# An encoder block on one core: output weights' last quarter read and summed beside branch A's merge, tokens' low parts behind the first blocks' results, gate weights read ahead of head one

## The chip, the core and the metric

The kernel runs on one core of a Trainium2 chip. The core has five engines that run side by side and meet through semaphores: TensorE (PE in the profile) for matrix products, VectorE (DVE), ScalarE (ACT), GpSimd (POOL), and SyncE (SP), which here only issues DMA transfers. Each engine works through its own instructions in order. The metric is device time in microseconds (us) of the whole program.

## The reference

One encoder layer over 1024 tokens and 16 meta tokens put ahead of them, width 1024, in float32:

```
h   = concat(meta, x)
p   = rms_norm(h) @ w_in                    # qa, ka, va, qb, kb, vb, gate a, gate b
y_a = differential attention, 4 heads       # two softmaxes subtracted, per-head norm
y_b = windowed attention, 8 heads, 2 key/value heads, window 128, sinks
m   = sigmoid(ga) * (y_a @ w_branch_a) + sigmoid(gb) * (y_b @ w_branch_b)
h   = h + m @ w_out
h   = h + (silu(n @ w_gate) * (n @ w_up)) @ w_down      # n = rms_norm(h), inner width 2816
out = rms_norm(h), without the meta tokens
```

## The kernel before, in words

Every matrix product is made of float32 values split in two: ACT copies the value into a rounded "high part" (line 112) and VectorE or POOL subtracts that from the value for the "low part" (line 113). Three products (high by high, high by low, low by high) then stand for one in float32. A product of 512 columns by 128 contracted rows is three matmuls, and four contracted chunks make twelve, summed in one PSUM bank.

The stages follow each other on TensorE: projections and windowed attention; the heads of differential attention, with the gate projections filling in between; branch B's merge and branch A's merge; the output projection; the feed-forward network, up and down. The order on TensorE is the program's order in most stages (`manual_schedule`). On the other engines and on SP's queue of transfers, a planner decides it when the kernel is compiled; buffers of a pool are handed on as their readers finish.

*The merges (from line 859).* For each of eight columns of 128 outputs (`o`) and each half of the tokens, `gated` reads the stored gate from DRAM into one of four buffers (`GT_BUFS`), ACT applies the sigmoid (line 862), and TensorE multiplies branch weights by the branch's result (line 551). VectorE then multiplies gate and product (line 874 in branch B, 899 in branch A), and in branch A POOL adds that to branch B's share (line 900). `branch_w` reads one column of branch weights into a raw tile of a ring of five (`RING_RAW`) and splits it into one of seven buffers (`WB_BUFS`). `order_a` is the order of branch A's sixteen outputs. The banks of PSUM alternate between two groups of four (`ps_bank`, `ps_bank_t`).

*The output projection* uses seven products in place of eight (Strassen's scheme in Winograd's form). For it the four quarters of `w_out` are read as W11, W12, W21 and W22, and turned in place into the sums that the scheme needs: T2 = W22 - W11 (line 1110), W12 := W22 - W12 (line 1164), W21 := W21 - T2 (line 1166), each in four pieces of 128 by 512. W22 has its read at the eleventh output of branch A, into the space of branch A's first operand. The merged values get sums of the same kind (lines 908, 915, 916, 1162). `right_o` and `left_o` split the operands; line 1121 and line 1129 hold the matmuls.

*The feed-forward network* uses the same scheme with `product_f` (line 1218). The first four blocks run their first two products (1 and 2) ahead of the rest. `turn_f` transposes the normalised tokens and forms their sums; `split_t` splits these sums into the operands `t_5`, `t_6`, `t_7`, `t_4` of the products 5, 6, 7 and 4, at the steps that `SPLIT` names. `result` applies silu (line 1230) to the gate's product, and multiplies it by the up product (line 1235), which is what gives the product's PSUM bank free.

*The heads.* `prep` reads 128 columns of `w_in` into a buffer of two and splits them; `ensure` does so ahead for the next columns of `order`; `load_a` reads a head's operands; `fill` runs steps of the gate projections.

Of the kernel before, what the change touches and what calls it, by code (L numbers as in the profile page):

```python
# [19 lines left out]
P = 128  # L20
# [23 lines left out]
G_BUFS = 3  # L44
HOLD = 36
GT_BUFS = 4
WB_BUFS = 7
G_HEAD = 10
G_FIRST = 30

# [20 lines left out]
def encoder_block(ctx: ExitStack, tc: tile.TileContext, x, meta, norm_mix, w_in, lq1, lk1, lq2, lk2,  # L71
# [94 lines left out]

    queue = []

    def prep(col, name, p=None, lo_eng=None):
        w = wpool.tile([P, DC, P], F32, tag="w", name=f"w_{name}", bufs=2)  # L170
        nc.sync.dma_start(w, w_in[:, col:col + P].rearrange("(c p) n -> p c n", p=P))
        p, bufs = (p, 1) if p else (wpool, W_BUFS)
        wh = p.tile([P, DC, P], F32R, tag="wh", name=f"wh_{name}", bufs=bufs)
        wl = p.tile([P, DC, P], F32R, tag="wl", name=f"wl_{name}", bufs=bufs)
        split(wh, wl, w, lo_eng or nc.gpsimd)
        return wh, wl
# [530 lines left out]
    for n in range(AH * NT + T_LAG):  # L707
        scoring, turning = iter(()), iter(())
        if n < AH * NT:
            h, t = divmod(n, NT)  # L710
            if t == 0:
                if not h:
                    ensure(2)
                ld = load_a(h)
                fill(G_HEAD if h else G_FIRST)
            if t % 2 == 0:
                at_ = apool.tile([P, 9, 2, 256], F32R, tag="at", name=f"at{h}_{t}", bufs=AT_BUFS)
            s = [None, None]
            tiles.append((h, t, s, at_, ld[2]))
            scoring = scores_a(h, t, ld, s)  # L720
        if n >= T_LAG:
            turning = turn(tiles[n - T_LAG])
        for what in SLOTS if n < 3 * NT else SLOTS_LAST:
            if what == "s":
                next(scoring, None)
            elif what == "t":
                next(turning, None)
            elif what == "n":
                step_tail()
            else:  # L730
                fill(1)
        for _ in scoring:
            pass
        for _ in turning:
            pass
        if n >= T_LAG and tiles[n - T_LAG][1] % 2:
            tail.append(later(tiles[n - T_LAG]))
# [153 lines left out]
    obpools[1], close_ob = pool("obpool", "right")  # L891


    order_a = [(o, 0) for o in range(6)] + [(0, 1), (6, 0), (1, 1), (7, 0)] + [(o, 1) for o in range(2, DC)]
    for n, (o, half) in enumerate(order_a):
        if o not in ws_a:
            ws_a[o] = branch_w(ypool, o, w_ba, "a", None, nc.vector)
        gt, ps, tk = gated(1, o, half, ws_a[o], ya)
        nc.vector.tensor_tensor(gt, gt, ps, ALU.mult)
        nc.gpsimd.tensor_tensor(merged(o, half), gt, merged(o, half), ALU.add)  # L900
        if 4 <= n < 8:
            right_o(2, n - 4)
            left_o(1, n - 4)
        elif 10 <= n < 14:
            left_o(2, n - 10)
        if n in (6, 8, 10, 11):

            tt_v(a21[:, o], a11[:, o], a21[:, o], ALU.subtract)
        if n == 10:
            w22 = obpools["w22"] = block_pair(2, "m2", F32)[:, 0]  # L910
            load_wo(w22, 1, 1)
        if n >= 12:

            j = n - 12
            tt_v(asum[:, j], a22[:, j], a21[:, j], ALU.subtract)
            tt_v(a11[:, j], asum[:, j], a11[:, j], ALU.add)
# [187 lines left out]
    for i in range(2):  # L1104
        load_unit(i, 0, first_f[i])

    for j in range(4):
        if j % 2 == 0:
            t2[j // 2] = raw_tile(f"t2_{j}")
        tt_v(t2[j // 2][:, j % 2 * 512:j % 2 * 512 + 512], w22[:, j], w11[:, j], ALU.subtract)  # L1110

    order_t = ((7, 0), (7, 1), (7, 2), (4, 0), (7, 3), (4, 1), (4, 2), (4, 3))
    steps_o = [(p, j) for p in (1, 2, 6, 5, 3) for j in range(4)]
    set1 = [ps_bank(f"po_1_{u}") for u in range(4)]
# [27 lines left out]
    for n, (p, j) in enumerate(steps_o):  # L1142
        if (p, j) == (5, 0):
            sets_o[5] = sets_o[3] = [ps_bank_t(f"po_5_{u}") for u in range(4)]
        last = p in (5, 3) and j == 3
        if p in (5, 3) and j == 2:
            continue
        for u in range(4):
            for k in (2, 3) if last else (j,):
                product_o(p, k, u)  # L1150
            if (p, j) == (1, 3):

                nc.scalar.copy(set2[u], set1[u])
            elif j == 3:

                out_add(u + 4 * (p == 5), int(p > 2), sets_o[p][u])
                if p == 3:
                    norm_f(u)
        for k in (n - 1, n) if last else (n,):
            ahead(k)  # L1160
            if 4 <= k < 8:
                tt_v(a12[:, k - 4], a12[:, k - 4], asum[:, k - 4], ALU.subtract)
            elif 8 <= k < 12:
                tt_v(w12[:, k - 8], w22[:, k - 8], w12[:, k - 8], ALU.subtract)
            elif 12 <= k < 16:
                tt_v(w21[:, k - 12], w21[:, k - 12], t2[(k - 12) // 2][:, k % 2 * 512:k % 2 * 512 + 512], ALU.subtract)
    TURN_O = {2: 0, 3: 1, 4: 2, 5: 3, 6: 4}
    b11, b21, b22 = (block_pair(i, n, F32R) for i, n in enumerate(("b11", "b21", "b22")))
    for n, (p, u) in enumerate(order_t):
# [5 lines left out]
            turn_f(TURN_O[n])  # L1175
    prepare(2 * 2)
    close_late()
    close_ob()
    close_wo()
    close_keep()  # L1180
# [18 lines left out]
        for p in ps_:  # L1199
            split(t_ops[p][:, 0, :, cols], t_ops[p][:, 1, :, cols], sums_t[u][p], nc.vector)  # L1200

    st = {}

    def product_f(fp, p, i):
        op, b = ops.pop(("f", (fp, p, i))), b_ops[p]
        u = st.setdefault((i, fp), {})
        nm = f"{i}_{fp}"
        which = {1: "b1", 6: "b1", 7: "b1", 4: "b1", 2: "b2", 5: "b3", 3: "b3"}[p]
        late = N_KEPT <= fp < N_EARLY
        if p in (1, 5) or (late and p == 6):  # L1210
            u[which] = (ps_bank_t if p == 5 else ps_bank)(f"pg_{nm}_{p}")
        ps = u[which]
        if late and p == 6:

            nc.scalar.copy(ps, u[1])
        for c in range(4):
            for n, (x, y) in enumerate(((0, 0), (0, 1), (1, 0))):
                nc.tensor.matmul(ps, op[:, x, c, :], b[:, y, c, :], start=(p in (1, 5) and c == 0 and n == 0),  # L1218
                                 stop=(p in (4, 2, 3) and c == 3 and n == 2), skip_group_check=True)
        g = st.setdefault(("c", fp), {})  # L1220

        def result(key, src, other=None):

            if i == 0:

                c = g[key] = (p_tile if key == "11" and fp < N_EARLY else c_tile)(f"c_{nm}_{key}")
                if other is not None:
                    nc.vector.tensor_tensor(c, src, other, ALU.add)
                    src = c
                nc.scalar.activation(c, src, AF.Silu)  # L1230
            else:
                if other is not None:
                    nc.vector.tensor_tensor(other, src, other, ALU.add)
                    src = other
                nc.vector.tensor_tensor(g[key], g[key], src, ALU.mult)  # L1235

        if p == 1:

            u["b2"] = ps if late else ps_bank(f"pg_{nm}_2")
            if late:  # L1240
                u[1] = p_tile(f"p1_{nm}")
            nc.scalar.copy(u[1] if late else u["b2"], ps)
        elif p in (5, 6):
            u[p] = c_tile(f"p{p}_{nm}")
            nc.scalar.copy(u[p], ps)
        elif p == 2:
            result("11", ps)
        elif p == 7:
            result("22", ps, u[5])
        elif p == 3:  # L1250
            result("12", ps, u[6])
        else:
            result("21", ps)
            if i:

                a11, a21, a12, a22 = g["11"], g["12"], g["21"], g["22"]
                nc.sync.dma_start(a_d[1][fp], a11)
                s1, s2, s3, s4 = (c_tile(f"as{k}_{fp}") for k in range(1, 5))
                nc.vector.tensor_tensor(s1, a21, a22, ALU.add)
                nc.sync.dma_start(a_d[4][fp], a22)  # L1260
                nc.vector.tensor_tensor(s3, a11, a21, ALU.subtract)
                nc.sync.dma_start(a_d[7][fp], s3)
                nc.vector.tensor_tensor(s2, s1, a11, ALU.subtract)
                nc.sync.dma_start(a_d[5][fp], s1)
                nc.sync.dma_start(a_d[6][fp], s2)
                nc.vector.tensor_tensor(s4, a12, s2, ALU.subtract)
                nc.sync.dma_start(a_d[2][fp], a12)
                nc.sync.dma_start(a_d[3][fp], s4)

    TURN = {0: 5, 2: 6, 4: 7}  # L1270
    SPLIT = {2: (0, (6, 5)), 3: (1, (6, 5)), 5: (2, (6, 5)), 7: (3, (6, 5))} | {8 + u: (u, (7, 4)) for u in range(4)}
    for n in range(nf):
        prepare()
        if n in TURN:
            turn_f(TURN[n])
        if n in SPLIT:
            split_t(*SPLIT[n])
        if n == 11:
            close_h2()
            cp, close_cpool = pool("cpool")  # L1280
            cpools.append(cp)
# [157 lines left out]
```

## Time and profile before

| what | us |
|---|---|
| median of 3 runs | 1455.42 (1452.44 to 1456.17) |
| the profiled execution | 1455.01 |
| its span, first to last instruction | 1453.2 |
| TensorE busy | 1432.0 |
| VectorE busy | 893.5 |
| ScalarE busy | 675.6 |
| GpSimd busy | 471.6 |

Times in the rows are microseconds from the span's start. A row of the timeline gives the start, the duration, the engine (SPq is SP's queue of transfers), the line, the operation, the tiles written and read, their shapes and the number of instructions merged into the row; in brackets, how long the engine was idle before and what ended that. A wait gives the waiting line, what it waited for, the total, the number of times and the longest. A stretch gives busy time of each engine in it, then the clock that TensorE was granted (1.00 is full speed) and the share of the DMA engines. VectorE issues a short instruction about 0.6 us after the one before, though a row shows it as 0.67 to 0.69 us long; matmul ends are modelled.

### The profile page before, as it was taken

To read this page: it belongs to the slowest core of one execution; us is meant where nothing else is said; L and a number is where in the kernel's file an instruction comes from. 1 tells how busy PE (TensorE), PEld (TensorE's weight loads), DVE (VectorE), ACT (ScalarE), POOL (GpSimd) and SP (SyncE) were. 2 spreads that over 40 slices of the span, in tenths; PEclk is the share of its full clock that TensorE was granted. 3 is DMA by queue.
4 is the path that set the end of the run, shared out by engine and by line. 5 is a ranking of instruction groups with operands and counts; after the bars stand their busy time and mean duration, and the time that the engine had idled before them with its cause. 6 is when DMAs were issued, how large, how long until landed. Compare 5 with 4: busy or idle time off the path is not lost.

```text
span 1453.2 us, 20988 instructions
## 1 busy us (share of the span) xinstructions
PE 1432.0 (99%) x7327; PEld 1227.8 (84%) x7327; DVE 893.5 (61%) x1750; ACT 675.6 (46%) x1275; POOL 471.6 (32%) x460
## 2 busy tenths in 40 slices
PE   8999999999999999999999999999999999999997
PEld 7999989988898989888878878888888888888886
DVE  6456326627686868535777955654455543787567
ACT  6356336525554545455345844333333333444454
POOL 4143223313323232211513035454444452000444
PEclk9999999999999999999999999999999999999999
DMA  7334452373424242077341533433223333954343
GB/s 237 88 102 115 123 126 88 78 192 109 147 80 147 74 147 74 30 267 240 108 161 73 181 109 109 145 124 108 96 99 104 105 102 106 349 186 138 124 130 138
DMA packets 158618, 191.02 MB, mean 131 GB/s; under 512 B 16096, under 2 KB 103584, under 8 KB 158512
## 3 DMA queue, kind: packets, MB, share of 16 engines
q1 hardware_dynamic: 158512, 189.68, 41.1%
q8 instruction: 58, 0.95, 0.3%
q14 instruction: 48, 0.39, 0.1%
HBM read 129.14 MB, written 53.94 MB: 126 GB/s over the span
## 4 chain that ended last, share of the span: by engine, by line
PE 81%; DMA 6%; issue 4%; POOL 4%; DVE 3%; ACT 2%; SPq 1%; POOLq 0%; ACTq 0%; DVEq 0%
PE pg L1218 28%; PE pp_g L200 10%; PE pd L1314 8%; PE aps L607 4%; PE po L1121 4%; PE apy L649 3%; PE pp_va L200 3%; PE pp_ka L200 3%; PE pp_qa L200 3%; PE pp_qb L200 3%; POOL oa L113 3%; PE apt L636 2%; PE bpt L338 2%; PE bpy L344 2%; PE po L1129 2%
## 5 line engine op out<-in xcount | busy, mean ns | idle before, releaser
L1218 PE MATMUL pg<-t,wop 128*128 128x512 f32 x1056 | 242.4, 389 | 0.0
L1218 PEld LDWEIGHTS pg<-t,wop 128*128 128x128 f32 x1056 | 198.3, 188 | 41.1
L1314 PE MATMUL pd<-ob,oa 128*128 128x512 f32 x924 | 210.2, 389 | 1.2 <-DVE ob L113 0.7
L1314 PEld LDWEIGHTS pd<-ob,oa 128*128 128x128 f32 x924 | 173.3, 188 | 37.9 <-DVE ob L113 1.2
L113 POOL TENSOR_TENSOR wop<-wf,wop 128x512 fp32r<-128x512 f32 x114 | 150.4, 1320 | 165.8 <-ACT wop L112 153.9
L1218 PE MATMUL pg<-b,wop 128*128 128x512 f32 x792 | 184.2, 390 | 2.2 <-DVE c L1235 1.8
L1218 PEld LDWEIGHTS pg<-b,wop 128*128 128x128 f32 x792 | 148.2, 188 | 34.2 <-DVE c L1235 2.7
L113 POOL TENSOR_TENSOR wl_c<-w_c,wh_c 128x1024 fp32r<-128x1024 f32 x32 | 77.7, 2427 | 166.3 <-ACT wh_c L112 156.0
L112 ACT ACTIVATE wop<-wf 128x512 fp32r<-128x512 f32 x128 | 80.8, 633 | 81.4 <-PE pg L1218 53.6
L618 ACT ACTIVATE as<-as,amn 128x1040 f32<-128x1040 f32 x64 | 74.5, 1164 | 72.7 <-DVE amn L613 72.4
L200 PE MATMUL pp_g<-hT_hi,wh_c 128*128 128x512 f32 x256 | 101.3, 396 | 0.0
L200 PE MATMUL pp_g<-hT_lo,wh_c 128*128 128x512 f32 x256 | 100.9, 394 | 0.0
L200 PE MATMUL pp_g<-hT_hi,wl_c 128*128 128x512 f32 x256 | 100.9, 394 | 0.0
L113 POOL TENSOR_TENSOR oa<-ra,oa 128x512 fp32r<-128x512 f32 x33 | 44.0, 1335 | 171.1 <-ACT oa L112 169.7
L112 ACT ACTIVATE oa<-ra 128x512 fp32r<-128x512 f32 x77 | 48.7, 632 | 108.1 <-PE pd L1314 51.3
L607 PE MATMUL aps<-ak,aq 128*128 128x352 f32 (+1 forms) x384 | 92.7, 326 | 0.4 <-DVE amn L613 0.4
L990 DVE TENSOR_TENSOR s<-wf,wf 128x512 f32<-128x512 f32 x22 | 15.7, 715 | 117.0 <-DMA wf<-in_w_ff_up_dram 70.1
L607 PEld LDWEIGHTS aps<-ak,aq 128*128 128x128 f32 x384 | 69.6, 188 | 14.8 <-DVE amn L613 0.9
L613 DVE CUSTOM_DVE_ANT_0 as<-aps,dist,amn 128x352 f32<-128x352 f32 (+1 forms) x128 | 71.3, 563 | 10.2 <-PE aps L607 8.1
L325 POOL TENSOR_SCALAR bs<-bs,bdn 128x432 f32<-128x432 f32 (+1 forms) x64 | 37.0, 597 | 85.4 <-DVE bdn L323 64.1
L613 DVE CUSTOM_DVE_ANT_0 as<-aps,dist,far_a 128x352 f32<-128x352 f32 x64 | 37.1, 579 | 42.8 <-PE aps L607 42.7
L621 POOL TENSOR_SCALAR as<-as,adn,neglam 128x1040 f32<-128x1040 f32 x32 | 38.9, 1217 | 75.2 <-DVE adn L619 75.2
(270 smaller groups left out, 3040.4 us busy)
## 6 DMA issues: line engine op xcount, KB each, us to landing
ra<-aop SPq DMA_DIRECT2D x77, 256.0 KB, 2.6
w_c<-in_w_in_dram SPq DMA_DIRECT2D x33, 512.0 KB, 3.9
wf<-in_w_ff_gate_dram SPq DMA_DIRECT2D x25, 512.0 KB, 3.5
wf<-in_w_ff_up_dram SPq DMA_DIRECT2D x25, 512.0 KB, 3.6
aop<-as SPq DMA_DIRECT2D x44, 256.0 KB, 2.0
aop<-c SPq DMA_DIRECT2D x33, 256.0 KB, 2.0
g_d<-gate_stage SPq DMA_DIRECT2D x32, 256.0 KB, 2.0
gt<-g_d SPq DMA_DIRECT2D x32, 256.0 KB, 4.1
```

The source lines that it names most:

```text
L112: nc.scalar.activation(hi, src, AF.Copy)
L113: lo_eng.tensor_tensor(lo, src, f32(hi), ALU.subtract)
L200: nc.tensor.matmul(ps[:, :n], a[:, c, :], b[:, c, at:at + n], start=(c == 0 and i == 0), stop=(c == DC - 1 and i == 2))
L325: nc.gpsimd.tensor_scalar(st[:, r, :W], st[:, r, :W], dn[:, r:r + 1], 1.0, ALU.mult, ALU.mult)
L607: nc.tensor.matmul(ps[:, :n], qs[m][:, t * P:(t + 1) * P], ks[m][:, vv, k0:k0 + n], start=(vv == 0), stop=(vv == 1))
L613: nc.vector.tensor_tensor_reduce(s[m][:, a:b], ps[:, a - k0:b - k0], far_by, slope, low, ALU.add, ALU.min, mn[:, m, i + j:i + j + 1])
L618: nc.scalar.activation(s[m][:, 0:L], s[m][:, 0:L], AF.Exp, bias=low, scale=-1.0, accum_out=dn[:, m:m + 1])
L621: (nc.gpsimd if t % 4 in COMBINE_POOL else nc.vector).tensor_scalar(s[1][:, 0:L], s[1][:, 0:L], dn[:, 1:2], neglam, ALU.mult, ALU.mult)
L649: nc.tensor.matmul(py[:, cols], v[:kp, a, k, :], at_[:kp, k, b, :], start=(k == 0 and j == 0), stop=(k == 8))
L1121: nc.tensor.matmul(sets_o[p][u], oa[:, a, u * P:(u + 1) * P], ob[:, b, :], start=(p in (1, 5) and j == 0 and k == 0), stop=(p in (2, 3) an ...
L1218: nc.tensor.matmul(ps, op[:, x, c, :], b[:, y, c, :], start=(p in (1, 5) and c == 0 and n == 0), stop=(p in (4, 2, 3) and c == 3 and n == ...
L1314: nc.tensor.matmul(ps[u], oa[:, a, u * P:(u + 1) * P], ob[:, b, :], start=(p in (1, 2, 5) and j == 0 and k == 0), stop=(p in (2, 3, 4) and ...
```

## The change

There are three parts. First, W22 gets a buffer of its own (`w22`, pool `w22pool`) and is read as branch A's merge begins; the twelve sums T2, W12 and W21 are placed behind the multiplications of outputs 3 to 6 and 8 to 11 (`issue_after` puts VectorE's instructions of the block behind the one named). `WB_BUFS` goes from 7 to 6; the order of the sixteen outputs changes a little, and so do the outputs behind which `a21` is subtracted. Second, the splits of the tokens' sums no longer come at steps 2 to 11 token by token, but operand by operand, behind the last multiplication of a result (`given[-1]`): operand 6 at step 4, 5 at step 8, 7 and 4 at step 12; the second extra block takes its bank from the other group of four, and the pool `cpool` opens at step 16 instead of 11. Third, `prep` can use weights that `preload` has read, and `preload` is called for the next columns of `order` before the first head's operands are read.

```
-WB_BUFS = 7
+WB_BUFS = 6
...
+    raw_w = {}
+    def preload(col):
+        w = raw_w[col] = wpool.tile([P, DC, P], F32, tag="w", name=f"w_c{col}", bufs=2)
+        nc.sync.dma_start(w, w_in[:, col:col + P].rearrange("(c p) n -> p c n", p=P))
     def prep(col, name, p=None, lo_eng=None):
-        w = wpool.tile([P, DC, P], F32, tag="w", name=f"w_{name}", bufs=2)
-        nc.sync.dma_start(w, w_in[:, col:col + P].rearrange("(c p) n -> p c n", p=P))
+        if col not in raw_w:
+            preload(col)
+        w = raw_w.pop(col)
...
                     ensure(2)
+                    preload(order[0])
                 ld = load_a(h)
...
-    order_a = [(o, 0) for o in range(6)] + [(0, 1), (6, 0), (1, 1), (7, 0)] + [(o, 1) for o in range(2, DC)]
+    order_a = [(o, 0) for o in range(5)] + [(0, 1), (5, 0), (1, 1), (6, 0), (2, 1), (7, 0)] + [(o, 1) for o in range(3, DC)]
+    w22pool, close_w22 = pool("w22pool", "right")
+    w22 = obpools["w22"] = w22pool.tile([P, 4, 512], F32, name="w22")
+    load_wo(w22, 1, 1)
     for n, (o, half) in enumerate(order_a):
...
-        nc.vector.tensor_tensor(gt, gt, ps, ALU.mult)
+        mult = nc.vector.tensor_tensor(gt, gt, ps, ALU.mult)
         nc.gpsimd.tensor_tensor(merged(o, half), gt, merged(o, half), ALU.add)
...
-        if n in (6, 8, 10, 11):
+        if n in (5, 7, 9, 11):
             tt_v(a21[:, o], a11[:, o], a21[:, o], ALU.subtract)
-        if n == 10:
-            w22 = obpools["w22"] = block_pair(2, "m2", F32)[:, 0]
-            load_wo(w22, 1, 1)
+        with tc.issue_after(mult.ins):
+            if 3 <= n < 7:
+                j = n - 3
+                if j % 2 == 0:
+                    t2[j // 2] = raw_tile(f"t2_{j}")
+                tt_v(t2[j // 2][:, j % 2 * 512:j % 2 * 512 + 512], w22[:, j], w11[:, j], ALU.subtract)
+                tt_v(w12[:, j], w22[:, j], w12[:, j], ALU.subtract)
+            elif 8 <= n < 12:
+                j = n - 8
+                tt_v(w21[:, j], w21[:, j], t2[j // 2][:, j % 2 * 512:j % 2 * 512 + 512], ALU.subtract)
...
-    for j in range(4):
-        if j % 2 == 0:
-            t2[j // 2] = raw_tile(f"t2_{j}")
-        tt_v(t2[j // 2][:, j % 2 * 512:j % 2 * 512 + 512], w22[:, j], w11[:, j], ALU.subtract)
...
-            elif 8 <= k < 12:
-                tt_v(w12[:, k - 8], w22[:, k - 8], w12[:, k - 8], ALU.subtract)
-            elif 12 <= k < 16:
-                tt_v(w21[:, k - 12], w21[:, k - 12], t2[(k - 12) // 2][:, k % 2 * 512:k % 2 * 512 + 512], ALU.subtract)
...
-    st = {}
+    st, given = {}, []
...
-            u[which] = (ps_bank_t if p == 5 else ps_bank)(f"pg_{nm}_{p}")
+            u[which] = (ps_bank_t if p == 5 or fp == 2 else ps_bank)(f"pg_{nm}_{p}")
...
-                nc.vector.tensor_tensor(g[key], g[key], src, ALU.mult)
+                given.append(nc.vector.tensor_tensor(g[key], g[key], src, ALU.mult))
...
-    SPLIT = {2: (0, (6, 5)), 3: (1, (6, 5)), 5: (2, (6, 5)), 7: (3, (6, 5))} | {8 + u: (u, (7, 4)) for u in range(4)}
+    SPLIT = {4: (6,), 8: (5,), 12: (7, 4)}
...
-        if n in SPLIT:
-            split_t(*SPLIT[n])
-        if n == 11:
+        for p in SPLIT.get(n, ()):
+            with tc.issue_after(given[-1].ins):
+                for u in range(4):
+                    split_t(u, (p,))
+        if n == 16:
             close_h2()
```

In the changed kernel the lines are shifted: branch A's multiplication is line 911 and POOL's add 912, the branch matmuls are line 558, the sums lines 927, 928 and 931, the projection's matmuls lines 1136 and 1144, the feed-forward matmuls line 1232, silu line 1244 and the multiplication line 1249.

More of the change, by code (lines that the diff above doesn't have):

```diff
@@ L1177, in encoder_block @@
     close_late()
+    close_w22()
     close_ob()
```

## The prediction

> **What bounds the kernel now.** I read the page first, then TensorE's waits, busy time by stretches around each long wait, and the timeline there.
>
> ```profile
> span 1453.2 us, 20988 instructions
> PE 1432.0 (99%) x7327; PEld 1227.8 (84%) x7327; DVE 893.5 (61%) x1750; ACT 675.6 (46%) x1275; POOL 471.6 (32%) x460
> ```
>
> TensorE is busy all but 21 us. The change adds and removes no matmul, so it can only move TensorE's waits, which the view of waits lists by the waiting line and by what ended the wait (total, times, longest):
>
> ```profile
> PE po L1121 <- DVE gt L899: 3.4, 1, 3.4
> PE apt L636 <- DVE as L624: 2.1, 1, 2.1
> ...
> PE pg L1218 <- DVE c L1235: 1.8, 2, 1.4
> ...
> PE pg L1218 <- ACT pg L1242: 0.3, 1, 0.3
> ```
>
> The first lies where branch A's merge passes into the output projection, the second at the first attention head, the last two in the first feed-forward blocks. Busy time by stretches (columns: PE, PEld, DVE, ACT, POOL, granted clock, DMA share, GB/s) gives the first one's full price:
>
> ```profile
> 330.00:340.00 10.00, 7.42 (x39) 5.99 (x38) 5.70 (x23) 5.67 (x10) 3.89 (x4) 1.00 0.54 176
> ...
> 720.00:730.00 10.00, 6.62 (x29) 5.18 (x29) 9.39 (x14) 0.63 (x1) 7.98 (x5) 1.00 0.25 79
> 730.00:740.00 10.00, 10.00 (x38) 8.04 (x38) 10.00 (x16) 4.74 (x9) 1.17 (x1) 0.83 0.75 275
> 740.00:750.00 10.00, 10.00 (x46) 8.29 (x45) 5.51 (x10) 5.28 (x10) 0.00 (x0) 1.00 0.74 251
> ```
>
> 3.4 us idle, then a clock of 0.83 over the next 10 us: 38 matmuls instead of 46, which at 10/46 = 0.22 us each are 1.7 us more. So this stop costs 5.1 us. The 2.1 us wait at the head (in 330 to 340) is not followed by a slower clock, so the drop sets in somewhere between 2.1 and 3.4 us of idling. What causes the stop is read from the timeline:
>
> ```profile
> 680.33 43.74 PE L551 MATMUL ppa<-ya,wbha 128*128 128x512 f32 x192
> 683.02 2.50 DVE L113 TENSOR_TENSOR ya<-raw_ya,ya 128x512 fp32r<-128x512 f32 x4 [1.67 <-ACT ya L112]
> 709.27 0.39 SPq L856 DMA_DIRECT2D m<-in_w_out_dram  x1
> 714.99 2.50 DVE L1110 TENSOR_TENSOR t<-m,m 128x512 f32<-128x512 f32 x4 [1.06 <-DMA m<-in_w_out_dram]
> 717.40 1.28 DVE L1164 TENSOR_TENSOR w<-m,w 128x512 f32<-128x512 f32 x2
> 721.02 0.68 DVE L899 TENSOR_TENSOR gt<-gt,ppa 128x512 f32<-128x512 f32 x1
> 721.77 7.48 POOL L900 TENSOR_TENSOR m<-gt,m 128x512 f32<-128x512 f32 x4 [8.57 <-DVE gt L899]
> 728.08 0.63 ACT L862 ACTIVATE gt<-gt 128x512 f32<-128x512 f32 x1 [11.03 <-DMA gt<-g_d]
> 728.74 0.69 DVE L899 TENSOR_TENSOR gt<-gt,ppa 128x512 f32<-128x512 f32 x1 [0.61 <-ACT gt L862]
> 729.48 5.77 PE L1121 MATMUL po<-ob_o,oa_o 128*128 128x512 f32 x17 [3.38 <-DVE gt L899]
> ```
>
> VectorE waits for W22 (read at 709.27), makes the twelve sums of L1110, L1164 and L1166, and only at 721.02 multiplies the twelfth of the merge's sixteen outputs. POOL's adds come late, the four gate buffers come free late, the last gate lands for 728.08, and TensorE lacks the PSUM bank that the last multiplication (728.74) gives back.
>
> **Part one: W22 early, the sums beside the merge.** The 1 MB read and the twelve sums stay; they are moved to between the multiplications of outputs 3 to 11. That takes away the stop above: -5.1 us. What is late next is branch A's weights. Before, the last of their eight reads went out at 677.93 (row below), ahead of the merge's first matmul at 680.33. In the compiled order of the changed kernel (one weight buffer fewer, and two ring buffers held by the T2 sums), the last four stand here on SP's queue, which waits in order:
>
> ```
> gt_4_0 [waits Pool]   gt_0_1 [Pool]   gt_5_0 [Pool]
> wbra (column 4)
> gt_1_1 [Pool]   gt_6_0 [Pool]
> wbra (column 5)   wbra (column 6)   wbra (column 7)
> ```
>
> So column 4, needed by the fifth output (call outputs n = 0 to 15), is read only after gate n=6 has a buffer, which is after POOL's add of n=2; column 5, needed by n=6, only after gate n=8, after POOL's add of n=4. That such queue waits are real, and what a link costs:
>
> ```profile
> SPq L861 <- POOL m L900: 38.0, 12, 11.1
> gt<-g_d SPq DMA_DIRECT2D x23, 256.0 KB, 3.1
> wbra<-in_w_branch_a_dram SPq DMA_DIRECT2D x8, 256.0 KB, 4.9
> 674.63 0.34 SPq L861 DMA_DIRECT2D gt<-g_d  x1
> 677.93 0.37 SPq L543 DMA_DIRECT2D wbra<-in_w_branch_a_dram  x1
> 686.54 0.62 ACT L112 ACTIVATE wbha<-wbra 128x512 fp32r<-128x512 f32 x1
> 689.54 0.67 DVE L899 TENSOR_TENSOR gt<-gt,ppa 128x512 f32<-128x512 f32 x1
> 690.14 0.68 DVE L113 TENSOR_TENSOR ob_o<-w,ob_o 128x512 fp32r<-128x512 f32 x1
> 690.30 1.68 POOL L900 TENSOR_TENSOR m<-gt,m 128x512 f32<-128x512 f32 x1 [2.43 <-DVE gt L899]
> 690.75 1.78 DVE L113 TENSOR_TENSOR oa_o<-m,oa_o 128x512 fp32r<-128x512 f32 x1
> 693.20 2.92 POOL L900 TENSOR_TENSOR m<-gt,m 128x512 f32<-128x512 f32 x2 [1.23 <-DVE gt L899]
> ```
>
> *First new stop.* An output takes 43.74/16 = 2.73 us, so n=4 is due at 680.33 + 4 x 2.73 = 691.3. POOL's add of n=2 is the first of the two at 693.20 and ended there at about 694.7 (half of 2.92 later). After, it ends at about 693.3: VectorE has lost the weight split (the wbha split, 0.6) that stood ahead of the second multiplication, the third can come one operation behind it, and POOL goes straight from its second add (ends 690.30 + 1.68 = 692.0) to the third (1.3). Then 0.4 us of queue for the gate, the weight read issued at 693.7, landed 3.3 us later (between the rows' 3.1 and 4.9, and nearer the first, for only one gate is ahead of it): 697.0, and ACT's split 0.6: 697.7. TensorE stops for 6.4 us. Lower end: output 2 ends at 688.5, and 0.7 + 1.3 + 0.4 + 3.1 + 0.6 later is 694.6: 3.3. Upper end, the add at 694.7 and 4.9 for the read: 9.3.
>
> *Second.* n=4 runs to 697.7 + 2.7 + 1.7 (low clock) = 702.1, and n=5, whose column 0 is there, to 704.8. Column 5 waits for n=4's multiplication (0.7), its add (1.3, and 0.5 of hand-overs), the gate ahead (0.4), the read (3.3) and the split (0.6): 702.1 + 6.8 = 708.9. TensorE stops for 4.1 us (3.4 without hand-overs and with 3.1 for the read; 5.7 with 4.9). Columns 6 and 7 go out right behind and aren't late.
>
> *Clock.* The drop came with a 3.4 us stop before, and both new ones are longer: 2 x 1.7 = 3.4 us. Ends: 0, if the drop is over before the matmuls resume, and 2 x 3.4.
>
> *End of the merge.* The last multiplication now stands behind the sums of n=12 to 14. Each of these outputs brings three sums (0.6 each), a POOL add that blocks them (1.3) and the multiplication (0.6): 3.7 us against TensorE's 2.73, so VectorE falls 2.9 us behind over three outputs. The matmuls end at 724.1 + 6.4 + 4.1 + 3.4 = 738.0; the multiplication begins at 740.9 and ends 0.7 later, while TensorE can run on for 2.0 us (before: from 724.07 to the stop at 726.1). Stop: 1.5 us, ends 0 and 3.4 (what it was).
>
> The W22 read itself is covered: it stands between gates n=2 and n=3, so it goes out about 681, takes 5.7 us (709.27 to 714.99) and is there by 687, before n=3's multiplication and the first sum behind it. If it were late, VectorE would stand at its first sum with n=4's multiplication queued behind it, and the adds and gates behind that.
>
> **Part two: tokens' low parts behind the first blocks' results.**
>
> ```profile
> 820.00:830.00 10.00, 9.27 (x43) 7.23 (x43) 10.00 (x18) 9.53 (x17) 0.00 (x0) 1.00 0.63 182
> 830.00:840.00 10.00, 8.84 (x40) 6.97 (x38) 10.00 (x18) 7.72 (x14) 0.00 (x0) 1.00 0.38 125
> 684.98 1.66 ACT L112 ACTIVATE ob_o<-w 128x512 fp32r<-128x512 f32 x3
> 821.64 0.64 ACT L112 ACTIVATE wop<-wf 128x512 fp32r<-128x512 f32 x1 [0.24 <-DMA wf<-in_w_ff_up_dram]
> 822.29 1.28 ACT L1230 ACT_TABLE_LOAD   x1
> 823.59 0.60 ACT L1230 ACTIVATE c<-pg 128x512 f32<-128x512 f32 x1
> 824.24 3.04 PE L1218 MATMUL pg<-b,wop 128*128 128x512 f32 x12
> 827.67 11.17 PE L1218 MATMUL pg<-b,wop 128*128 128x512 f32 x48 [0.39 <-DVE c L1235]
> 840.28 15.96 PE L1218 MATMUL pg<-b,wop 128*128 128x512 f32 x69 [1.44 <-DVE c L1235]
> ```
>
> VectorE is full for 20 us, and two products wait for a bank that its results free (0.39, 1.44). With the splits behind the results, and block 2 on the other four banks, both waits go: -1.8. But in the compiled order of ACT four more instructions (three of the tokens' high parts and a copy) stand ahead of the table load at 822.29, each 1.66/3 = 0.55 us, together 2.2, of which some 0.5 fits where ACT waits at 821.64 and before the load. The product at 824.24 starts the moment the first silu (823.59 + 0.60) ends, so it starts 1.7 us later: +1.7. Sum -0.1, ends -1.8 (the four hidden) and +1.7 (the waits stay in another place). The deferred splits are first read twelve products of 2.7 us after the one at 824.24, 32 us later; VectorE's backlog of at most eight splits more, 5 us, is covered by that.
>
> **Part three: gate weights ahead of head one.** In the compiled order this read keeps its place and its waits on SP's queue, and no engine's order differs before the merge of branch B. Worth 0; the 2.1 us wait at the head stays (ends 0 and -2.1).
>
> **Sum**, against the profiled execution's 1455.01 us (1.8 outside its span; 0.4 below the median of 1455.42): -5.1 + 6.4 + 4.1 + 3.4 + 1.5 - 0.1 = +10.2, so 1465.2, rounded 1465.
>
> **Rivals.** *The port, not the weights.* If columns 4 and 5 came in time, VectorE's sums and POOL's adds would still meet: at 690.75 a VectorE operation with both inputs in SBUF took 1.78 instead of 0.68, ending 0.55 after POOL's add (690.30 + 1.68). From 683.0 on (the ya splits), sixteen adds of 1.3 and some 43 such operations of 0.6 ahead of the last multiplication make 47 us, so it comes at 730 with all sixteen multiplications hidden under adds, at 740 with none. With 733.5, between them, TensorE, out of work at 726.1, stops about 8 us with a clock drop of 1.7: 1455 + 8 + 1.7 - 5.1 = 1459.6. It decides as soon as the last multiplication is later than 729. [...] For this rival: the durations; against it as the main cause: the reads' places in the queue.
>
> *Faster.* One mechanism: the weight reads are early enough, because the POOL adds that hold SP's queue end far sooner than before. Column 4 must be split by 691.3, so its read issued by 687.4, when only the first add is done. If so, 5.1 and 1.8 us go: 1448. It decides where the new stops stay below 5 us together; the lower ends above already give 6.7.
>
> *No visible change.* Stops at their lower ends (3.3 + 3.4), no clock drop, no end stop: 1455.0 - 5.1 + 6.7 - 0.1 = 1456.5.
>
> **Chances.** Late weights 0.78 (own range 1459 to 1470), the port alone 0.07, no change 0.06, faster 0.09. A measurement here tells 0.3% (4.4 us) from nothing. Late weights stay below that in 0.03 and the port's case in half: slower 0.79, same 0.12, faster 0.09. The range reaches down to 1457, past the port's case, and up to 1470 (reads of 4.9 us, +3.2, and +1.8 in part two).
>
> **What would show it.** Right: TensorE waiting at L558 twice inside branch A's merge, some 6 and 4 us, released by ACT's split of wbha; the granted clock below 1.00 after each; the po wait on L911 at 0 to 2 us; waits of L1232 on the multiplication L1249 gone, and one on ACT's silu instead. Wrong: the merge running without a wait (then part one gives its 5.1 us), or reads of columns 4 and 5 landing before 691.

## The result, and the profile after

The changed kernel takes 1464.32 us (median of 6 runs, 1462.56 to 1467.95), the kernel before 1454.48 in as many runs beside it (1452.44 to 1459.09): a ratio of 1.0069, 95% interval 1.0051 to 1.0086, so 7.4 to 12.5 us slower. The profiled execution took 1465.3 us. Its page, the span and the first part:

```profile
span 1463.5 us, 20998 instructions
PE 1436.9 (98%) x7327; PEld 1232.8 (84%) x7327; DVE 905.4 (62%) x1750; ACT 676.8 (46%) x1275; POOL 474.3 (32%) x460
```

The span has grown by 10.3 us, TensorE's busy time by only 4.9: the rest is waiting, and the 4.9 is the same number of matmuls at a lower clock (0.991 over the whole span, 0.998 before). The view of TensorE's waits (waiting line, what it waited for, total, times, longest) of the changed kernel:

```profile
PE ppa L558 <- ACT wbha L112: 8.9, 2, 4.9
...
PE pg L1232 <- ACT c L1244: 1.6, 1, 1.6
...
PE po L1136 <- DVE gt L911: 1.1, 1, 1.1
```

The first row is new: two stops inside branch A's merge (L558), for weights that ACT had not yet split. The stop at the output projection has shrunk from 3.4 to 1.1 us, and in the feed-forward network one wait for the silu (L1244) stands where two waits for VectorE stood. The timeline of the changed kernel from the merge's start shows where the weights were:

```profile
679.90 11.04 PE L558 MATMUL ppa<-ya,wbha 128*128 128x512 f32 x48
680.10 0.38 SPq L865 DMA_DIRECT2D w<-in_w_out_dram  x1
688.04 2.93 POOL L912 TENSOR_TENSOR m<-gt,m 128x512 f32<-128x512 f32 x2 [2.43 <-DVE gt L911]
691.37 0.43 SPq L550 DMA_DIRECT2D wbra<-in_w_branch_a_dram  x1
695.16 0.63 ACT L112 ACTIVATE wbha<-wbra 128x512 fp32r<-128x512 f32 x1
695.85 8.06 PE L558 MATMUL ppa<-ya,wbha 128*128 128x512 f32 x24 [4.90 <-ACT wbha L112]
701.95 1.67 POOL L912 TENSOR_TENSOR m<-gt,m 128x512 f32<-128x512 f32 x1 [8.11 <-DVE gt L911]
704.07 1.49 SPq L550 DMA_DIRECT2D wbra<-in_w_branch_a_dram  x3
707.20 0.63 ACT L112 ACTIVATE wbha<-wbra 128x512 fp32r<-128x512 f32 x1
707.88 30.80 PE L558 MATMUL ppa<-ya,wbha 128*128 128x512 f32 x120 [3.97 <-ACT wbha L112]
741.78 3.47 PE L1136 MATMUL po<-ob_o,oa_o 128*128 128x512 f32 x14 [1.05 <-DVE gt L911]
```

Column 4's read leaves SP at 691.37, 0.4 us after POOL's add of output 2 ends (688.04 + 2.93 = 690.97), when TensorE has already run out of columns. Columns 5, 6 and 7 leave from 704.07, 0.4 us after the next add that a gate in front of them waits for (701.95 + 1.67 = 703.62). The merge began 0.4 us earlier than before (679.90 against 680.33) and the output projection went on 12.3 us later (741.78 against 729.48). Busy time by stretches of the changed kernel (PE, PEld, DVE, ACT, POOL, granted clock, DMA share, GB/s):

```profile
690.00:700.00 10.00, 5.10 (x15) 3.68 (x14) 5.88 (x7) 4.05 (x7) 2.62 (x2) 0.70 0.35 105
700.00:710.00 10.00, 5.99 (x20) 4.08 (x19) 8.04 (x10) 2.52 (x4) 3.32 (x2) 0.84 0.43 130
710.00:720.00 10.00, 10.00 (x36) 7.94 (x36) 5.61 (x8) 2.53 (x4) 3.35 (x2) 0.78 0.09 30
```

The clock fell after both stops. At 46 matmuls per 10 us, the 15 + 20 + 36 matmuls here need 15.4 us; TensorE was busy for 21.1. So the low clock cost 5.7 us, besides the 8.9 us of standing still.

Behind the merge nothing more is lost: from 741.78 to the product after the first silu (836.21, below) it is 94.4 us, before it was 94.8 (729.48 to 824.24), and from there to the end of the span 627.3 against 629.0.

### The profile page after: what moved, and what is told of

Read it like the earlier page. It is cut to its first block, busy times and chain, and to the rows that moved or that the text cites. A ratio compares the mean times of both kernels' runs of the same rounds, so it can differ in the third digit from the quotient of the medians.

```text
span 1463.5 us, 20998 instructions
## 1 busy us (share of the span) xinstructions
PE 1436.9 (98%) x7327; PEld 1232.8 (84%) x7327; DVE 905.4 (62%) x1750; ACT 676.8 (46%) x1275; POOL 474.3 (32%) x460
## 4 chain that ended last, share of the span: by engine, by line
PE 87%; POOL 4%; issue 3%; DVE 2%; DMA 2%; ACT 1%; SPq 0%; POOLq 0%; DVEq 0%; ACTq 0%
PE pg L1232 28%; PE pp_g L207 12%; PE pd L1331 8%; PE aps L614 4%; PE ppa L558 4%; PE po L1136 4%; PE apy L656 3%; PE pp_qb L207 3%; PE pp_va L207 3%; PE pp_ka L207 3%; PE pp_qa L207 3%; POOL oa L113 3%; PE apt L643 2%; PE bpt L345 2%; PE bpy L351 2%
## 5 line engine op out<-in xcount | busy, mean ns | idle before, releaser
L1010 DVE TENSOR_TENSOR s<-wf,wf 128x512 f32<-128x512 f32 x22 | 15.4, 699 | 109.7 <-DMA wf<-in_w_ff_up_dram 60.9
L620 DVE CUSTOM_DVE_ANT_0 as<-aps,dist,amn 128x352 f32<-128x352 f32 (+1 forms) x128 | 71.3, 564 | 10.2 <-PE aps L614 8.1
L322 DVE CUSTOM_DVE_ANT_0 bs<-bps,tbx,nsink 128x432 f32<-128x432 f32 (+1 forms) x64 | 38.4, 625 | 41.4 <-PE bps L320 38.4
```

The lines of the kernel that those rows point to most:

```text
L322: nc.vector.tensor_tensor_reduce(st[:, r, :W], ps[:, :W], tb, 2.0 ** -(4 * g + r + 1), nsink[:, 4 * g + r:4 * g + r + 1], ALU.add, ALU.min ...
L620: nc.vector.tensor_tensor_reduce(s[m][:, a:b], ps[:, a - k0:b - k0], far_by, slope, low, ALU.add, ALU.min, mn[:, m, i + j:i + j + 1])
```

## The experiments

The kernel before stood at 1454.08 us beside the first four kernels and at 1454.47 beside the last four. Each profile is one execution, and single executions of one kernel lie up to some 5 us to either side of the median (the kernel before: 1449.2 to 1459.8); so medians give the times, and profiles the places.

**1. Weights first.** The changed kernel with the weight reads taken out of the queue's tail:

```
+    for o in range(1, 6):
+        ws_a[o] = branch_w(ypool, o, w_ba, "a", None, nc.vector)
+    raw67 = raw_tile("wbra_67")
+    for k, o in enumerate((6, 7)):
+        nc.sync.dma_start(raw67[:, k * 512:k * 512 + 512]..., w_ba[:, o * P:(o + 1) * P]...)
     for n, (o, half) in enumerate(order_a):
         if o not in ws_a:
-            ws_a[o] = branch_w(ypool, o, w_ba, "a", None, nc.vector)
+            ws_a[o] = ypool.tile(...); split(ws_a[o][:, 0], ws_a[o][:, 1], <half of raw67>, nc.vector)
```

> The changed kernel, with branch A's weight columns 1 to 5 read and split ahead of the merge's loop, and columns 6 and 7 read into one raw tile there (their splits stay at their outputs), so that no weight read stands behind T2's tiles or behind a gate that waits for POOL. All sums stay where the change put them. Theory (late weights): the two TensorE waits for wbha (4.9 and 4.0 us) and the clock lost behind them (some 5.6 us) go, 14.5 us off 1464.3, so about 1450; as VectorE and POOL lose the 9 us of standstill in which they caught up, the stop at the merge's end may grow from 1.1 to at most 3.4 us plus 1.7 of clock, which gives 1450 to 1454. Rival (the port): VectorE's sums and POOL's adds exclude each other, the last multiplication comes near 733 and TensorE stands some 8 us at the first output product: 1457 to 1460, with the multiplication as the releaser.

Measured: 1457.3 us (ratio to before 1.0020, 1.0008 to 1.0033), 7 us less than the changed kernel, above the theory's range and within the rival's. Waits of this kernel, and around its merge's end VectorE's rows (L918 is the multiplication, L942, L943 and L1185 the sums of the merged values), one of POOL and one of TensorE:

```profile
PE po L1143 <- DVE gt L918: 4.0, 1, 4.0
PE pg L1239 <- ACT c L1251: 1.6, 1, 1.6
...
PE ppa L558 <- DVE wbha L113: 0.8, 1, 0.8
```

```profile
724.54 0.68 DVE L942 TENSOR_TENSOR m<-m,m 128x512 f32<-128x512 f32 x1
725.14 0.68 DVE L918 TENSOR_TENSOR gt<-gt,ppa 128x512 f32<-128x512 f32 x1
725.74 0.68 DVE L943 TENSOR_TENSOR m<-m 128x512 f32<-128x512 f32 x1
726.34 1.75 DVE L1185 TENSOR_TENSOR m<-m,m 128x512 f32<-128x512 f32 x1
...
728.61 0.68 DVE L918 TENSOR_TENSOR gt<-gt,ppa 128x512 f32<-128x512 f32 x1
...
725.90 1.64 POOL L919 TENSOR_TENSOR m<-gt,m 128x512 f32<-128x512 f32 x1 [1.83 <-DVE gt L918]
729.34 4.84 PE L1143 MATMUL po<-ob_o,oa_o 128*128 128x512 f32 x13 [4.04 <-DVE gt L918]
```

The waits for ACT's split of wbha are gone (0.8 us for its low part is left), so late weight reads made the two new stops: that theory held. But its time did not: the stop at the output projection came back with 4.0 us. One output takes VectorE 725.14 to 728.61, 3.5 us, and TensorE 2.7. In that time stands one sum of 1.75 us, held until POOL's add is over (725.90 + 1.64 = 727.54). So the rival's mechanism is real, at half the size that the prediction gave it (4.0 us, not 8).

**2. T2 later.** The changed kernel, where only T2 and W21 go back to the output projection; the weight reads are not touched:

```
             if 3 <= n < 7:
                 j = n - 3
-                if j % 2 == 0:
-                    t2[j // 2] = raw_tile(f"t2_{j}")
-                tt_v(t2[j // 2][...], w22[:, j], w11[:, j], ALU.subtract)
                 tt_v(w12[:, j], w22[:, j], w12[:, j], ALU.subtract)
-            elif 8 <= n < 12:
-                tt_v(w21[:, j], w21[:, j], t2[j // 2][...], ALU.subtract)
...
```

> The changed kernel with T2 (four sums) put back to the output projection's beginning and W21 (four sums) back to its steps; W22's own buffer, its early read, the W12 sums beside the merge, and six weight buffers stay. Nothing is done to the weight reads themselves. Theory: it is T2's two tiles in the ring of five that hold back the reads of columns 4 to 7; without them both wbha waits are gone and the end stop is at most 1 us: 1448 to 1451. Rival: six weight buffers in place of seven, or W22's 1 MB read in the queue, hold the weights back; then waits of some 4 to 5 us on wbha stay, and the time is 1459 to 1465.

Measured: 1454.89 us (1.0013, 0.9998 to 1.0027). Waits of this kernel, the last row of SP's queue that reads branch A's weights, and the stretch with the longer stop:

```profile
PE ppa L558 <- DVE wbha L113: 3.2, 1, 3.2
...
PE po L1135 <- DVE gt L911: 2.3, 1, 2.3
```

```profile
677.90 0.38 SPq L550 DMA_DIRECT2D wbra<-in_w_branch_a_dram  x1
```

```profile
700.00:710.00 10.00, 6.84 (x31) 5.34 (x30) 10.00 (x13) 4.74 (x9) 4.99 (x3) 1.00 0.24 80
```

All weights are read by 677.90 again, with six buffers and W22's read in the queue: it was T2's two tiles, taken in order from the ring of five that the weights use, that had pushed the reads back. The time was missed by 4 us all the same, because VectorE became the limit: it is full for the 10 us of the last row, and the low part of column 6, the last step before TensorE can use it, waits its turn there (3.2 us). Part of what fills VectorE is the very sums that the edit puts later: behind no `issue_after`, the planner queued all eight between the multiplications of outputs 0 and 3. Two of these rows, of T2 and of W21 (the second held by POOL's adds: 2.88 us for two sums, where the four of the first took 2.48):

```profile
687.05 2.48 DVE L1124 TENSOR_TENSOR t<-w,m 128x512 f32<-128x512 f32 x4
694.26 2.88 DVE L1179 TENSOR_TENSOR w<-w,t 128x512 f32<-128x512 f32 x2
```

So this run shows what held back the reads, and not what the sums would cost at the output projection.

**3. Part two alone, on the kernel before** (`SPLIT`, `issue_after`, the bank of the second extra block, `cpool`):

```
-    SPLIT = {2: (0, (6, 5)), 3: (1, (6, 5)), 5: (2, (6, 5)), 7: (3, (6, 5))} | {8 + u: (u, (7, 4)) for u in range(4)}
+    SPLIT = {4: (6,), 8: (5,), 12: (7, 4)}
```

> The kernel before with part two of the change alone (tokens' low parts behind results, bank of the second extra block, cpool later). Prediction's step: the two waits of the first feed-forward products on VectorE (1.8 us) go, the first silu comes some 1.7 us later: -0.1 in sum. The changed kernel's trace has one wait of 1.6 us on the silu there and no other, -0.6: 1453.5 to 1454.5. Rival: VectorE's stretch of 20 full microseconds was worth more than its two waits, and 2 to 3 us go: 1451.5 to 1452.5.

Measured: 1452.84 us (1.0000, 0.9985 to 1.0015), between the two ranges named. Its waits:

```profile
PE po L1121 <- DVE gt L899: 2.2, 1, 2.2
PE pg L1218 <- ACT c L1230: 1.6, 1, 1.6
```

One wait for another, as in the changed kernel; the medians differ by nothing that can be told. The first row is a finding of its own: with the merge of the kernel before, the old stop was 2.2 us in this execution, not 3.4.

**4. Part three alone, on the kernel before** (`preload`):

> The kernel before with part three alone (gate weights read ahead of head one). Prediction's step: the read keeps its place in the queue, 0 us: 1454.5, and where TensorE reaches the head as early as in the profile of before, its wait of some 2 us for the first head's transposes stays. Rival: the preloading takes that wait away, 2.1 to 2.5 us: 1452. In the changed kernel the wait is gone, but its first projections also ran 2.9 us later; which of the two it was is seen from the start and the wait of this run.

Measured: 1452.34 us (0.9999, 0.9983 to 1.0016). The median is near the rival's 1452, but the runs lie between 1449.5 and 1459.8, and the interval leaves some 2.4 us either way open; what decides is the wait. Two waits of this kernel and the stretch behind the second:

```profile
PE po L1129 <- DVE gt L907: 3.5, 1, 3.5
...
PE apt L643 <- DVE as L631: 2.1, 1, 2.1
```

```profile
340.00:350.00 10.00, 8.77 (x44) 7.94 (x45) 8.53 (x29) 5.04 (x11) 1.62 (x3) 0.83 0.12 43
```

The wait at the head stays with the preloading, and it is missing without it in experiment 3. So that it is missing in the changed kernel's profile is not part three's doing. What differs between executions is when SP gets to the gate weights' read: in the kernel before (first row, with the wait), in experiment 3 (second, without it) and here (third, with it):

```profile
327.28 0.38 SPq L171 DMA_DIRECT2D w_c<-in_w_in_dram  x1
```

```profile
325.11 0.38 SPq L171 DMA_DIRECT2D w_c<-in_w_in_dram  x1
```

```profile
329.22 0.38 SPq L173 DMA_DIRECT2D w_c<-in_w_in_dram  x1
```

ACT splits these weights ahead of the first head's exponentials (in the kernel before at 331.92, the first exponential at 333.35). Why SP gets there later in some executions was not settled: between two reads ahead of this one (lines 589 and 590 of the kernel before) lie 3.1 us in the kernel before, 1.4 in experiment 3 and 2.7 in experiment 4.

**5. Weights first, the merged values' sums last.** Experiment 1, with `asum`, `a11` and `a12` queued behind the merge's last multiplication:

```
-        if n >= 12:
-            j = n - 12
-            tt_v(asum[:, j], a22[:, j], a21[:, j], ALU.subtract)
-            tt_v(a11[:, j], asum[:, j], a11[:, j], ALU.add)
+    with tc.issue_after(mult.ins):
+        for j in range(4):
+            tt_v(asum[:, j], a22[:, j], a21[:, j], ALU.subtract)
+            tt_v(a11[:, j], asum[:, j], a11[:, j], ALU.add)
...
+                with tc.issue_after(mult.ins):
                     tt_v(a12[:, k - 4], a12[:, k - 4], asum[:, k - 4], ALU.subtract)
```

> Experiment 1 (weights first), with the twelve sums of the merged values (asum, a11, a12) queued on VectorE behind the merge's last multiplication; T2, W12 and W21 stay beside the merge. In experiment 1 these three sums per output, one of them held up by POOL's add (1.75 us), made 3.5 us per output at the end against TensorE's 2.7, and TensorE stood 4.0 us at the first output product. Theory (VectorE is late because of what stands ahead of the last multiplications): that stop falls to at most 1 us and its clock loss goes, 4 to 5 us off experiment 1's 1457.3: 1452 to 1453. Rival: VectorE is already behind from outputs 4 to 8 (busy without a gap from 690 to 710), and the stop stays at 2 us or more: 1455 or above.

Measured: 1450.7 us (0.9981, 0.9968 to 0.9994), 6.6 us less than experiment 1 and 1.3 less than the theory's range. The stop at the output projection is gone altogether, as this stretch of it shows:

```profile
720.00:730.00 10.00, 10.00 (x46) 8.29 (x45) 7.54 (x11) 2.42 (x4) 5.46 (x4) 1.00 0.69 190
```

So the 4.0 us of experiment 1 were these sums, in front of the last multiplications.

**6. Sums last, without an early read.** The kernel before, with T2 and W12 behind the last multiplication, where W22 is read as late as ever:

```
+    with tc.issue_after(mult.ins):
         for j in range(4):
             ...
             tt_v(t2[j // 2][...], w22[:, j], w11[:, j], ALU.subtract)
...
             elif 8 <= k < 12:
+                with tc.issue_after(mult.ins):
                     tt_v(w12[:, k - 8], w22[:, k - 8], w12[:, k - 8], ALU.subtract)
```

> The kernel before, where T2 and W12 (and with them W21, which needs T2) are queued on VectorE behind the merge's last multiplication; W22 is read where it was, seven weight buffers, no other part of the change. Theory: the old stop (3.4 us and 1.7 of clock in the profile of before) came from the order on VectorE, not from the late read: it falls to at most 1 us, 3.5 to 5 us off 1454.1: 1449 to 1451. Rival: the late read itself is the limit, VectorE only moves its sums into the output projection's way, and a wait for sixth-product operands takes the place: 1453 to 1455.

Measured: 1450.94 us (0.9984, 0.9971 to 0.9997). Its waits:

```profile
PE pg L1220 <- DVE c L1237: 2.1, 2, 1.4
...
PE po L1122 <- DVE gt L899: 0.7, 1, 0.7
```

The old stop was a matter of order on VectorE: an edit of a few lines takes it to 0.7 us, and no wait for later operands comes instead.

**7. All sums last, and part two with ACT held too.** Experiment 6 with the sums of experiment 5, and with part two, which differs in this line:

```
-            with tc.issue_after(given[-1].ins):
+            with tc.issue_after(given[-1].ins), tc.issue_after(silus[-1].ins):
                 for u in range(4):
                     split_t(u, (p,))
```

> Experiment 6 with the merged values' sums (asum, a11, a12) queued behind the last multiplication too, and part two with ACT's splits of the tokens' sums queued behind the silu (in part two alone three of them stood ahead of the first silu, and TensorE waited 1.6 us for it). Theory: no stop at the output projection (at most 0.5), and the first silu is no longer late, so no wait above 0.5 us at the feed-forward's first products: 1446 to 1449. Rival: VectorE's 24 sums pile up at the output projection's beginning and the operands for its third product come late, 2 us or more: 1450 or above.

Measured: 1448.72 us (0.9964, 0.9950 to 0.9977). VectorE behind the last multiplication (first row) in this kernel:

```profile
723.15 0.69 DVE L899 TENSOR_TENSOR gt<-gt,ppa 128x512 f32<-128x512 f32 x1 [2.03 <-PE ppa L551]
723.75 2.99 DVE L914 TENSOR_TENSOR m<-m,m 128x512 f32<-128x512 f32 x3
726.66 2.48 DVE L1110 TENSOR_TENSOR t<-m,m 128x512 f32<-128x512 f32 x4
729.07 2.48 DVE L1166 TENSOR_TENSOR w<-m,w 128x512 f32<-128x512 f32 x4
```

VectorE now waits for TensorE there (2.03), not TensorE for VectorE. TensorE has no wait at the output projection and none at the first silu.

**8. Both.** Experiment 5 with the hold on ACT of experiment 7:

> Experiment 5 (weights first, the weights' sums beside the merge, the merged values' sums last) with part two's ACT splits queued behind the silu as in experiment 7. Theory: no stop at the weights, at most 1 us at the output projection, none at the silu: 1448 to 1451, level with experiment 7 or up to 2 us above it, since W12, W21 and T2 still meet POOL's adds. Rival: with the sums beside the merge the early read gains over experiment 7, as VectorE is freer at the output projection: 1445 to 1446.

Measured: 1447.46 us (0.9960, 0.9943 to 0.9976), 17 us below the changed kernel and 7 below the kernel before, half a microsecond under the range expected. One wait is left in the merge:

```profile
PE ppa L558 <- DVE wbha L113: 1.7, 1, 1.7
```

Experiments 7 and 8 cannot be told apart (1448.72 with runs from 1445.62 to 1451.73, 1447.46 with 1447.04 to 1448.09), so the early read and its buffer bring nothing that can be told beside what the order on VectorE brings without them.

## Why the prediction was right, step by step

The profiled execution of the changed kernel is 10.3 us longer than that of before, and the medians differ by 9.8; the prediction's sum was +10.2. Parts two and three alone measure as nothing (experiments 3 and 4), so part one, which was not run alone, carries it, by the mechanism named: experiments 1 and 2 take the late reads away from the changed kernel, each in another way, and both stops for ACT's split go. Of the terms, two were off in opposite directions:

- *The old stop, -5.1.* Its 3.4 us of idling went (the 1.05 us now there are counted below), and the clock from 740 to 750 is 1.00. But the 5.1 is one execution's price: the same merge had 2.2 us and no drop in experiment 3 (1.00 from 730 to 740), and 3.5 us in experiment 4 (0.83).
- *First new stop, +6.4; it was 4.9.* The queue, the add that holds it and the split were right. Mis-sized was the end of POOL's add of output 2: 693.3 against 690.97. The prediction moved up the multiplication of output 2 alone and left output 1's where it was; but those of outputs 0 and 1 came 2.2 us earlier too (683.19 and 687.29, before 685.43 and 689.54), behind earlier splits of `ya` (680.78, before 683.02). The read then took a little longer than the 3.3 taken (issued 691.37, split at 695.16).
- *Second new stop, +4.1; it was 4.0.* The chain from the multiplication of output 4 to the split of column 5 was of the length worked out.
- *Clock, +3.4; it was 5.7.* This is the term that was too small. The price of 1.7 per stop was one row's (a stop of 3.4 us). Here, at the pace of the 48 matmuls ahead of the stops (11.04 us), the 24 behind the first would take 5.5 us and the 120 behind the second 27.6; they took 8.06 and 30.80. That is 2.5 and 3.2 us, in sum within the prediction's upper end of 6.8. Nor does the drop set in "somewhere between 2.1 and 3.4 us of idling", as the last section shows.
- *End of the merge, +1.5; it was 1.05.* VectorE's sums and the add that holds them (a sum of 1.77 us in place of 0.68 at 738.75, the multiplication at 741.05) did make the last multiplication late; experiments 1 and 5 show that this stop belongs to the sums of the merged values.
- *Part two, -0.1.* The silu was late by 1.6 (predicted 1.7) since ACT's splits stand ahead of its table load, and the two waits on VectorE went. Experiments 5 and 8 show the cause: they differ only in these splits, which experiment 8 holds behind the silu, and the wait of 1.6 us is there in experiment 5 and gone in 8. Rows around it in the changed kernel:

```profile
834.27 1.28 ACT L1244 ACT_TABLE_LOAD   x1
835.56 0.60 ACT L1244 ACTIVATE c<-pg 128x512 f32<-128x512 f32 x1
836.21 14.13 PE L1232 MATMUL pg<-b,wop 128*128 128x512 f32 x61 [1.62 <-ACT c L1244]
```

- *Part three, 0.* Right in time (0.9999), but "the 2.1 us wait at the head stays" did not hold for the profiled execution: it was missing there, and in experiments 1, 3, 5 and 6 too, with and without part three. That was a difference between executions, and another of the opposite sign stood at the start. The stretch in which the first projections run, of the changed kernel and of the kernel before:

```profile
10.00:20.00 10.00, 7.22 (x35) 6.08 (x34) 9.22 (x11) 6.99 (x10) 6.27 (x5) 0.74 0.89 285
```

```profile
10.00:20.00 10.00, 7.24 (x55) 6.16 (x53) 9.22 (x11) 6.49 (x10) 6.26 (x5) 1.00 0.82 273
```

The changed kernel's execution started at the lower clock, 20 matmuls behind. That the sum agrees to 0.1 us with the profile is thus partly luck: the first stop was 1.5 too long, the clock 2.3 too short.

Of the rivals, *the port* is a true cost that the late weights covered (what is measured is that VectorE's sums and POOL's adds hold each other up, 1.75 us in place of 0.68 in experiment 1; through what, no run shows): with the weights in time it gave 1457.3 (experiment 1; 1459.6 was worked out), and in the changed kernel VectorE had the 8.9 us of standstill to catch up in (that this is why its last stop is 1.05 us and not 4.0 is argued, not shown). *Faster* needed more than early weight reads: it came with the sums out of the way (1450.7, experiment 5, and 1447.5, experiment 8).

## What to carry to other kernels

Where an engine stalls behind work that is merely ready sooner, first queue that work behind what the critical engine waits for; here this took a few lines, while moving the read that the work needs took buffers and places in a queue from others. When a tile is taken from a ring that prefetches use, look at which reads now stand behind it, and behind which waits of the queue. And price a stop of TensorE by its idling plus a range for the clock (here 0 to 3.2 us), not by the one drop that a profile shows.

## What the runs showed of the hardware

- *The clock's price is not set by the stop's length alone.* A wait of 2.1 us was followed by a clock of 0.83 in experiment 4, and by 1.00 in the kernel before (row below); 3.2 us by 1.00 (experiment 2); in the changed kernel the 4.9 us cost 2.5 and the 4.0 us 3.2. What sets it besides, no run here shows. The stretch behind the head's wait in the kernel before:

```profile
340.00:350.00 10.00, 10.00 (x62) 9.04 (x60) 9.54 (x35) 5.93 (x12) 2.57 (x3) 1.00 0.07 26
```

- *VectorE's sums against POOL's adds.* A sum that started while POOL added was held: 1.75 us in place of 0.68 in experiment 1 (726.34), over 0.55 us after POOL's add. It went the other way too: in the changed kernel POOL's add took 1.67 us at 701.95, where a sum had started 0.16 us ahead of it, and 1.29 at 732.11, where none had.
- *The start scatters.* The same first matmuls ran at 1.00 in one execution and at 0.74 in another, which alone moves the start by some 2.6 us (20 matmuls at the pace of 55 in 7.24 us). At the first head a wait of 0 to 2.1 us comes on top, depending on when SP reaches a read; it does not follow the start alone, for experiment 4 began at 0.70 and waited 2.1 us too.
